# Closing down-projection on one core: the squares of a finished block issued one chunk after its addition to the residual

## The chip, the cores and the metric

The kernel runs on one core of a Trainium2 chip. The metric is the device time of one execution in microseconds (us); before the change three runs gave 2178.75, 2179.22 and 2181.02 us, median 2179.22 us. One further execution was taken by the hardware profiler; it took 2178.91 us, of which the profile's span (first to last instruction) is 2177.0 us.

## The reference, cut to what matters

The program is a two-layer decoder trunk on 256 tokens with model width 2048, in float32: a gMLP token mixer and a convolutional feed-forward network, a shared key/value side, forgetting attention, a second feed-forward network, and a final RMSNorm. The change lies in the end of it:

```python
def rmsnorm(x, g):
    xf = x.astype(jnp.float32)
    r = lax.rsqrt(jnp.mean(xf * xf, axis=-1, keepdims=True) + EPS)
    return (xf * r).astype(x.dtype) * g
...
        h = h + conv_ffn(rmsnorm(h, f_norm[l]), f_w_up[l], f_conv_w[l],
                         f_conv_b[l], f_w_down[l])
...
    return rmsnorm(h, final_norm)
```

So after the last down-projection (a 256 x 5632 by 5632 x 2048 product) each token's row is added to the residual, the sum of its 2048 squares is taken, and the row is multiplied by the gains of the final norm and by one factor per token.

## The kernel before

**A stream of weight chunks.** All weights pass through one loop, `Stream.run`. An item of it is a chunk of weights, 128 partitions x 1024 float32, 512 KB. For item i the loop does four things in the order in which the instructions then stand in every engine's queue: SyncE issues the load of item i + 6 (L78); item i + 3 is *split*, which means that ScalarE rounds the raw chunk `raw` to a part `whi` of lower precision (L110) and VectorE writes the remainder `wlo` = `raw` - `whi` (L111); TensorE multiplies item i (L212: products of the rounded and remainder parts of weights and activations); and then every pending generator is *advanced* to its next `yield`. Generators hold all the other work (evictions from PSUM, norms, attention). A `yield` in such a generator thus means: the rest is issued one chunk later, behind the split of the next item. No scheduler moves anything. Every engine takes its queue in the order in which the loop wrote it.

**Rooms.** There are four `whi` and four `wlo` buffers, so item i + 3 is split into those of item i - 1, as soon as TensorE is done with that item. There are four `raw` buffers.

**The closing stage.** The second down-projection takes the tokens as the stationary operand and makes its output in blocks of 512 columns. Blocks 0, 1 and 2 mix two kinds of items. A *plain* chunk is split as above and gives 24 matrix multiplications of 256 columns. A *seven* chunk is one load but two items: VectorE first makes sums of its weights into a room (L490, L492, L493); the first item is the split of the raw weights (`whi` L88, `wlo` L89, 768 wide, 9 multiplications), the second item the split of the sums (L88 and L89 again, 1024 wide, 12 multiplications). Block 0 has one seven chunk among 22, near its end; blocks 1 and 2 have eight each, in the order plain, plain, seven, plain, seven, plain, plain, seven and so on. Block 3 is two short blocks of 256 columns of plain chunks, and the last of them is written out by a separate function, `output`.

**What happens to a finished block.** The generator `sums_into_residual` adds the seven chunks' sums to the residual `h` in four steps (L569 to L578). Then the generator `final`, for each of the two token halves tb = 0, 1, adds the block's PSUM to `h` on VectorE and squares it on ScalarE with a sum along the row, both issued in one step (`add_block`, L435 and L436); in the next step VectorE multiplies by the gains (L449). Five blocks end like this; the last, in `output`, calls `add_block` too.

**The sums of the activations.** Before the first seven chunk, a generator `all_sums` makes sums of the activation tiles in four rounds (`sums_of_blocks`, L469 to L478): additions on VectorE, then ScalarE rounds the result into a tile (L477) and VectorE writes the remainder (L478). The tile is called X in the profile; it is the stationary operand of the seven chunks.

Of the kernel before, what the change touches and what calls it, by code (L numbers as in the profile page):

```python
# [10 lines left out]
F32 = mybir.dt.float32  # L11
F32R = mybir.dt.float32r
I32 = mybir.dt.int32
AF = mybir.ActivationFunctionType
OP = mybir.AluOpType
AX = mybir.AxisListType

P = 128
D = 2048
T = 256  # L20
# [156 lines left out]
def build(ctx, tc, d, out):  # L177
    nc = tc.nc
# [3 lines left out]
    small = ctx.enter_context(tc.tile_pool(name="small", bufs=1))  # L182
# [228 lines left out]
    def by_token():  # L411

        return h.rearrange("p a b -> p (a b)").rearrange("p (t f) -> p t f", t=2)
# [17 lines left out]
    def add_block(tb, cols, ps, into):  # L431

        hh = by_token()[:, tb, cols]
        sq = small.tile([P, 2, T], F32, name="sq", tag="sq", bufs=2).rearrange("p a b -> p (a b)")
        nc.vector.tensor_tensor(hh, hh, ps, op=OP.add)  # L435
        nc.scalar.activation(sq[:, :ps.shape[1]], hh, AF.Square, accum_out=into)  # L436

    def final(blk):
        def done(ps):
            while state["summed"] < min(blk + 1, 3):  # L440
                yield
            ss = ph.keep("ss", [P, 2, 5])
            n = ps.shape[2]
            cols = slice(blk * 512, blk * 512 + n)
            for tb in range(2):
                add_block(tb, cols, ps[:, tb, :], ss[:, tb, blk:blk + 1])
                yield
                hh = by_token()[:, tb, cols]
                nc.vector.tensor_tensor(hh, hh, ph.keep("gains", [P, D])[:, cols], op=OP.mult)  # L449
                yield  # L450
            if blk == 3:
                v, nv = ph.keep("v", [P, 2]), ph.keep("nv", [P, 2])
                nc.vector.tensor_reduce(v, ss[:, :, :4], axis=AX.X, op=OP.add)
                nc.vector.tensor_scalar(v, v, 1.0 / D, EPS, op0=OP.mult, op1=OP.add)
                nc.vector.tensor_scalar(nv, v, -0.5, None, op0=OP.mult)
                nc.scalar.activation(warm, ones, AF.Sqrt)
        return done

    def block_sums():

        return X1.rearrange("p (q r) w -> p q (r w)", r=2).rearrange("p q (f l t) -> p q f l t", f=4, l=2)

    def sums_of_blocks(q, pair):

        H = ffn_h()
        x, f = (room().rearrange("p (q i t) -> p q i t", q=2, i=4) for _ in range(2))
        hi, lo = (block_sums()[:, q:q + 2, :, i, :] for i in range(2))
        hh = H[:, 2 * pair:2 * pair + 4, :].bitcast(F32)
        nc.vector.tensor_tensor(x.rearrange("p q i t -> p (q i t)").rearrange("p (k t) -> p k t", k=4),  # L469
                                hh[:, :, :T], hh[:, :, T:], op=OP.add)  # L470
        nc.vector.tensor_tensor(f[:, :, :2, :], x[:, :, 1:2, :].to_broadcast([P, 2, 2, P]), x[:, :, 0::3, :],
                                op=OP.subtract)
        yield
        nc.vector.tensor_tensor(f[:, :, 2, :], f[:, :, 1, :], x[:, :, 0, :], op=OP.subtract)
        nc.vector.tensor_tensor(f[:, :, 3, :], f[:, :, 2, :], x[:, :, 2, :], op=OP.add)
        yield
        nc.scalar.activation(hi, f, AF.Copy)  # L477
        nc.vector.tensor_tensor(lo, f, hi.bitcast(F32), op=OP.subtract)  # L478
        yield

    def all_sums():
        for _ in range(4):
            yield
        for q in range(0, len(SUMMED), 2):
            yield from sums_of_blocks(q, SUMMED[q])
# [312 lines left out]
    def ffn_h():  # L798
        ph.open(f"ffn{state['layer']}")
        return ph.keep("H", [P, KF, 2 * T], F32R)  # L800

    def room():
        return ph.temp("room", [P, CHUNK])
# [411 lines left out]
```

## Time and profile before

| | us |
|---|---|
| median of three runs | 2179.22 |
| the profiled execution | 2178.91 |
| its span | 2177.0 |
| TensorE busy | 2165.4 |
| VectorE busy | 1535.1 |
| ScalarE busy | 1163.4 |
| closing stage, about | 1932 to 2169 |

Busy time is the time in which the profile shows at least one instruction on the engine. In the rows of the timeline the columns are: start in us from the span's start, duration in us, engine, source line, operation, output <- inputs, matrix or tile shapes, count (neighbouring instructions of one kind are merged), and in brackets the idle time of the engine just before and what ended it. PE is TensorE, DVE VectorE, ACT ScalarE, SPq the queue of SyncE. In the rows of waits the columns are: the engine and line that waited, the engine and line that it waited for, us in total, how often, the longest.

### The profile page before, as it was taken

To read this page: it belongs to the slowest core of one execution; us is meant where nothing else is said; L and a number is where in the kernel's file an instruction comes from. 1 tells how busy PE (TensorE), PEld (TensorE's weight loads), DVE (VectorE), ACT (ScalarE), POOL (GpSimd) and SP (SyncE) were. 2 spreads that over 40 slices of the span, in tenths; PEclk is the share of its full clock that TensorE was granted. 3 is DMA by queue.
4 is the path that set the end of the run, shared out by engine and by line. 5 is a ranking of instruction groups with operands and counts; after the bars stand their busy time and mean duration, and the time that the engine had idled before them with its cause. 6 is when DMAs were issued, how large, how long until landed. Compare 5 with 4: busy or idle time off the path is not lost.

```text
span 2177.0 us, 45111 instructions
## 1 busy us (share of the span) xinstructions
PE 2165.4 (99%) x18689; PEld 2148.9 (99%) x18689; DVE 1535.1 (71%) x2188; ACT 1163.4 (53%) x1560; POOL 27.4 (1%) x46
## 2 busy tenths in 40 slices
PE   9999999999999999999999999999999999999998
PEld 9999999999999999999999999999999999999998
DVE  6696687777777745556787676678777777778874
ACT  6665555555555544444554665546555555554553
POOL 0000000000000000000001200000000000000000
PEclk9999999999999999999999999999999999999999
DMA  8686565565666566666778776567756565655574
GB/s 312 191 245 200 192 198 194 187 201 188 200 192 195 195 193 195 194 194 184 246 238 263 235 220 199 184 223 220 246 194 194 194 194 187 201 191 177 196 215 153
DMA packets 153230, 447.32 MB, mean 205 GB/s; under 512 B 25584, under 2 KB 44800, under 8 KB 152640
## 3 DMA queue, kind: packets, MB, share of 16 engines
q1 hardware_dynamic: 151488, 440.48, 63.1%
q0 software_dynamic: 1072, 3.41, 0.6%
q8 instruction: 146, 2.39, 0.5%
q10 hardware_dynamic: 464, 0.55, 0.1%
q14 instruction: 60, 0.49, 0.1%
HBM read 430.72 MB, written 13.65 MB: 204 GB/s over the span
## 4 chain that ended last, share of the span: by engine, by line
PE 99%; DVE 1%; DMA 0%; ACT 0%; SPq 0%; issue 0%; DVEq 0%; ACTq 0%
PE ps L212 97%; PE mp L1072 0%; DMA mlp_vt<-a_in_v 0%; DVE wlo L111 0%; ACT whi L110 0%; PE ps L1067 0%; PE ps L1066 0%; PE ps L1065 0%; PE mp L1071 0%; DVE wlo L89 0%; DVE h L435 0%; SPq L78 0%; ACT sq L436 0%; SPq L652 0%; DVE h L647 0%
## 5 line engine op out<-in xcount | busy, mean ns | idle before, releaser
L111 DVE TENSOR_TENSOR wlo<-raw,whi 128x1024 fp32r<-128x1024 f32 x761 | 923.7, 1219 | 390.6 <-ACT whi L110 386.9
L110 ACT ACTIVATE whi<-raw 128x1024 fp32r<-128x1024 f32 x761 | 800.8, 1058 | 674.3 <-PE ps L212 599.2
L212 PE MATMUL ps<-X,whi 128*128 128x256 f32 (+1 forms) x6476 | 824.0, 279 | 0.0
L212 PEld LDWEIGHTS ps<-X,whi 128*128 128x128 f32 x6476 | 776.2, 188 | 6.5
L212 PE MATMUL ps<-X,wlo 128*128 128x256 f32 x3328 | 445.3, 276 | 0.0
L212 PEld LDWEIGHTS ps<-X,wlo 128*128 128x128 f32 x3328 | 409.9, 188 | 1.6
L212 PE MATMUL ps<-whi,ffn_H 128*128 128x256 f32 (+1 forms) x1232 | 201.5, 277 | 0.5 <-ACT whi L110 0.4
L212 PE MATMUL ps<-whi,X 128*128 128x256 f32 (+1 forms) x1136 | 183.1, 279 | 0.4 <-ACT whi L110 0.4
L212 PEld LDWEIGHTS ps<-whi,ffn_H 128*128 128x128 f32 x1232 | 172.9, 188 | 1.3 <-ACT whi L110 0.9
L212 PE MATMUL ps<-ffn_H,whi 128*128 128x256 f32 x1408 | 173.9, 276 | 0.0
L822 DVE SCALAR_TENSOR_TENSOR ffn_room<-ffn_room,col 128x255 f32<-128x255 f32 x352 | 161.8, 481 | 6.4
L212 PEld LDWEIGHTS ps<-ffn_H,whi 128*128 128x128 f32 x1408 | 166.1, 188 | 0.0
L212 PE MATMUL ps<-whi,att_X 128*128 128x256 f32 (+2 forms) x970 | 164.3, 285 | 0.0
L212 PEld LDWEIGHTS ps<-whi,X 128*128 128x128 f32 x1136 | 155.0, 188 | 2.0 <-ACT whi L110 0.6
L212 PE MATMUL ps<-wlo,ffn_H 128*128 128x256 f32 (+1 forms) x615 | 139.2, 277 | 1.5 <-DVE wlo L111 1.5
L212 PEld LDWEIGHTS ps<-whi,att_X 128*128 128x128 f32 x970 | 135.3, 188 | 3.5
L388 DVE TENSOR_TENSOR ffn_room<-ps,rB 128x512 f32<-128x512 f32 x76 | 52.6, 692 | 116.1 <-PE ps L212 116.1
L818 ACT ACTIVATE ffn_room<-ffn_room,col 128x256 f32<-128x256 f32 x176 | 96.3, 595 | 50.0 <-DVE ffn_room L388 50.0
L212 PE MATMUL ps<-wlo,X 128*128 128x256 f32 (+1 forms) x566 | 116.7, 279 | 0.0
L212 PE MATMUL ps<-wlo,att_X 128*128 128x256 f32 (+2 forms) x476 | 105.4, 286 | 0.0
L212 PEld LDWEIGHTS ps<-wlo,ffn_H 128*128 128x128 f32 x615 | 101.1, 188 | 2.0 <-DVE wlo L111 1.9
L212 PE MATMUL ps<-ffn_H,wlo 128*128 128x256 f32 x704 | 94.1, 276 | 0.0
(196 smaller groups left out, 1518.0 us busy)
## 6 DMA issues: line engine op xcount, KB each, us to landing
raw<-up SPq DMA_DIRECT2D x352, 512.0 KB, 4.1
raw<-down SPq DMA_DIRECT2D x154, 512.0 KB, 4.2
raw<-a_in_u SPq DMA_DIRECT2D x32, 512.0 KB, 4.2
raw<-a_out SPq DMA_DIRECT2D x32, 512.0 KB, 3.9
raw<-b_q SPq DMA_DIRECT2D x32, 512.0 KB, 4.5
raw<-kvf_v SPq DMA_DIRECT2D x32, 512.0 KB, 4.9
raw<-b_g SPq DMA_DIRECT2D x32, 512.0 KB, 4.4
raw<-b_out SPq DMA_DIRECT2D x32, 512.0 KB, 4.0
```

The costliest lines, as they stand in the source:

```text
L110: self.nc.scalar.activation(h, raw, AF.Copy)
L111: self.nc.vector.tensor_tensor(l, raw, h.bitcast(F32), op=OP.subtract)
L212: nc.tensor.matmul(o, a, b, start=start, stop=stop, skip_group_check=True)
L388: nc.vector.tensor_tensor(a, src, rB[:, None, :].to_broadcast([P, 2, T]), op=OP.mult)
L818: nc.scalar.activation(c[:, m, :], a[:, m, :], AF.Identity, scale=w[2], bias=column(C_CONVB + l * 2 * KF + f))
L822: nc.vector.scalar_tensor_tensor(c[:, m, n:], a[:, m, :T - n], w[k], c[:, m, n:], op0=OP.mult, op1=OP.add)
```

## The change

Two generators have their `yield` statements moved; no instruction is added or taken away. In `final` the square is issued one chunk after the addition, and the multiplication by the gains in the step after that, together with the addition of the second half. The number of steps is the same. `output` still uses `add_block` as it was. In `sums_of_blocks` the remainder is issued one chunk after the rounding.

```diff
             for tb in range(2):
-                add_block(tb, cols, ps[:, tb, :], ss[:, tb, blk:blk + 1])
-                yield
                 hh = by_token()[:, tb, cols]
+                sq = small.tile([P, 2, T], F32, name="sq", tag="sq", bufs=2).rearrange("p a b -> p (a b)")
+                nc.vector.tensor_tensor(hh, hh, ps[:, tb, :], op=OP.add)
+                yield
+                nc.scalar.activation(sq[:, :n], hh, AF.Square, accum_out=ss[:, tb, blk:blk + 1])
+                yield
                 nc.vector.tensor_tensor(hh, hh, ph.keep("gains", [P, D])[:, cols], op=OP.mult)
-                yield
...
         nc.scalar.activation(hi, f, AF.Copy)
+        yield
         nc.vector.tensor_tensor(lo, f, hi.bitcast(F32), op=OP.subtract)
-        yield
```

Two lines more stand ahead of the later code, so line numbers above L450 are two higher in the changed kernel (L490 becomes L492, L578 becomes L580), the addition L435 is L448 there, the square L436 is L450, and the multiplication by the gains L449 is L452.

ScalarE's queue at the end of block 0, before:

```order
L110 ACTIVATE whi<-raw 128x1024
L436 ACTIVATE sq,ffn_ss<-h 128x512
L88 ACTIVATE whi<-raw 128x768
L88 ACTIVATE whi<-ffn_room 128x1024
L436 ACTIVATE sq,ffn_ss<-h 128x512
L110 ACTIVATE whi<-raw 128x1024 x2
```

and now:

```order
L110 ACTIVATE whi<-raw 128x1024
L88 ACTIVATE whi<-raw 128x768
L450 ACTIVATE sq,ffn_ss<-h 128x512
L88 ACTIVATE whi<-ffn_room 128x1024
L110 ACTIVATE whi<-raw 128x1024
L450 ACTIVATE sq,ffn_ss<-h 128x512
```

Each square stands one rounding later: the first behind the rounding of the next seven chunk's raw weights, the second behind the rounding of the plain chunk that follows that seven chunk. The end of block 1 reads the same.

VectorE's queue at the same place, before (`ffn_room` is the room of the weight sums):

```order
L435 TENSOR_TENSOR h<-h,ps 128x512
L490 TENSOR_TENSOR ffn_room<-raw 128x512
L492 TENSOR_TENSOR ffn_room<-raw,ffn_room 128x256
L493 TENSOR_TENSOR ffn_room<-raw,ffn_room 128x256
L89 TENSOR_TENSOR wlo<-raw,whi 128x768
L449 TENSOR_TENSOR h<-h,ffn_gains 128x512
L89 TENSOR_TENSOR wlo<-ffn_room,whi 128x1024
L435 TENSOR_TENSOR h<-h,ps 128x512
L111 TENSOR_TENSOR wlo<-raw,whi 128x1024
L449 TENSOR_TENSOR h<-h,ffn_gains 128x512
L111 TENSOR_TENSOR wlo<-raw,whi 128x1024
```

and now:

```order
L448 TENSOR_TENSOR h<-h,ps 128x512
L492 TENSOR_TENSOR ffn_room<-raw 128x512
L494 TENSOR_TENSOR ffn_room<-raw,ffn_room 128x256
L495 TENSOR_TENSOR ffn_room<-raw,ffn_room 128x256
L89 TENSOR_TENSOR wlo<-raw,whi 128x768
L89 TENSOR_TENSOR wlo<-ffn_room,whi 128x1024
L452 TENSOR_TENSOR h<-h,ffn_gains 128x512
L448 TENSOR_TENSOR h<-h,ps 128x512
L111 TENSOR_TENSOR wlo<-raw,whi 128x1024 x2
L452 TENSOR_TENSOR h<-h,ffn_gains 128x512
```

Both multiplications by the gains stand one remainder later; the additions stay where they were.

The last of the four rounds of activation sums, on VectorE, before:

```order
L475 TENSOR_TENSOR ffn_room<-ffn_room 128x2x128
L111 TENSOR_TENSOR wlo<-raw,whi 128x1024
L478 TENSOR_TENSOR X_74<-ffn_room,X_74 128x8x128
L490 TENSOR_TENSOR ffn_room<-raw 128x512
L492 TENSOR_TENSOR ffn_room<-raw,ffn_room 128x256
L493 TENSOR_TENSOR ffn_room<-raw,ffn_room 128x256
L89 TENSOR_TENSOR wlo<-raw,whi 128x768
L89 TENSOR_TENSOR wlo<-ffn_room,whi 128x1024
```

and now:

```order
L477 TENSOR_TENSOR ffn_room<-ffn_room 128x2x128
L111 TENSOR_TENSOR wlo<-raw,whi 128x1024
L492 TENSOR_TENSOR ffn_room<-raw 128x512
L494 TENSOR_TENSOR ffn_room<-raw,ffn_room 128x256
L495 TENSOR_TENSOR ffn_room<-raw,ffn_room 128x256
L89 TENSOR_TENSOR wlo<-raw,whi 128x768
L481 TENSOR_TENSOR X_74<-ffn_room,X_74 128x8x128
L89 TENSOR_TENSOR wlo<-ffn_room,whi 128x1024
```

The remainder X of the last round moved from ahead of the first seven chunk's weight sums to between its two weight remainders; in the first three rounds it moved behind one more `wlo` of a plain chunk. The queues of TensorE, GpSimd and SyncE are the same in both kernels.

More of the change, by code (lines that the diff above doesn't have):

```diff
@@ L445, in done @@
             for tb in range(2):
-                add_block(tb, cols, ps[:, tb, :], ss[:, tb, blk:blk + 1])
+                hh = by_token()[:, tb, cols]
+                sq = small.tile([P, 2, T], F32, name="sq", tag="sq", bufs=2).rearrange("p a b -> p (a b)")
+                nc.vector.tensor_tensor(hh, hh, ps[:, tb, :], op=OP.add)
                 yield
-                hh = by_token()[:, tb, cols]
+                nc.scalar.activation(sq[:, :n], hh, AF.Square, accum_out=ss[:, tb, blk:blk + 1])
+                yield
                 nc.vector.tensor_tensor(hh, hh, ph.keep("gains", [P, D])[:, cols], op=OP.mult)
-                yield
             if blk == 3:
```

## The prediction, made before the change was run

> **What bounds the kernel now.** I read the page first, then the waits of TensorE after 1900 us, then that engine's busy time in windows.
>
> ```profile
> span 2177.0 us, 45111 instructions
> PE 2165.4 (99%) x18689; PEld 2148.9 (99%) x18689; DVE 1535.1 (71%) x2188; ACT 1163.4 (53%) x1560; POOL 27.4 (1%) x46
> ...
> PE 99%; DVE 1%; DMA 0%; ACT 0%; SPq 0%; issue 0%; DVEq 0%; ACTq 0%
> ```
> ```profile
> PE ps L212 <- DVE wlo L111: 1.5, 2, 0.8
> PE ps L212 <- ACT whi L110: 0.4, 1, 0.4
> ```
> ```profile
> 1940.00:1980.00 40.00, 40.00 (x355) 40.00 (x355) 34.21 (x39) 19.93 (x20) 0.00 (x0) 1.00 0.62 204
> ...
> 2003.00:2007.00 4.00, 3.12 (x26) 2.73 (x25) 2.25 (x4) 3.36 (x5) 0.00 (x0) 1.00 0.20 79
> 2007.00:2061.00 54.00, 54.00 (x479) 54.00 (x478) 46.68 (x60) 27.63 (x30) 0.00 (x0) 1.00 0.63 206
> 2061.00:2066.00 5.00, 3.85 (x31) 3.45 (x31) 3.26 (x5) 3.35 (x5) 0.00 (x0) 1.00 0.30 97
> 2066.00:2120.00 54.00, 54.00 (x479) 54.00 (x479) 44.24 (x54) 28.06 (x30) 0.00 (x0) 1.00 0.71 216
> ```
>
> TensorE is the bound everywhere: 11.6 us of the span are outside its busy time. What the change can win is only what TensorE waits in the closing stage, and that is two places, the ends of blocks 0 and 1; the windows ahead, between and behind are full. The second number of a window is TensorE's busy time; the granted clock (third number from the end) is 1.00 in all five. Here are the two places on TensorE:
>
> ```profile
> 2004.77 0.89 PE L212 MATMUL ps<-whi,ffn_H 128*128 128x256 f32 x3
> 2006.42 0.50 PE L212 MATMUL ps<-wlo,ffn_H 128*128 128x256 f32 x2 [0.76 <-DVE wlo L111]
> ...
> 2063.31 0.28 PE L212 MATMUL ps<-whi,ffn_H 128*128 128x256 f32 x1
> 2063.98 0.50 PE L212 MATMUL ps<-whi,ffn_H 128*128 128x256 f32 x2 [0.39 <-ACT whi L110]
> 2065.24 0.50 PE L212 MATMUL ps<-wlo,ffn_H 128*128 128x256 f32 x2 [0.76 <-DVE wlo L111]
> ```
>
> In both, the last multiplication of a seven chunk (2004.77, the first of the three; 2063.31) is followed by a plain chunk, call it c: two multiplications with `whi`, then `wlo`. The pitch is 54.00 us / 479 = 0.113 us, so without a wait `wlo` of c would begin 3 x 0.113 = 0.34 us after the seven chunk's last one: at 2005.11 and 2063.65. It began at 2006.42 and 2065.24, that is **1.31 and 1.59 us late, 2.90 us together**.
>
> By busy time the loss reads smaller: 4.00 - 3.12 = 0.88 and 5.00 - 3.85 = 1.15 us, 2.03 together. In the Trainium skill, the page "Perfetto Trace Analysis" (opening note) calls matmul busy time a bad metric because matmuls are pipelined; the trace agrees, with 0.28 us shown for a multiplication whose pitch is 0.113 us, and by busy time the sum below would give 2.0 instead of 2.9 us. I take the starts, since they are what moves the end.
>
> Why c's remainder was late, on ScalarE and then VectorE:
>
> ```profile
> 1994.93 1.06 ACT L110 ACTIVATE whi<-raw 128x1024 fp32r<-128x1024 f32 x1 [1.66 <-PE ps L212]
> 1998.61 0.63 ACT L436 ACTIVATE sq<-h 128x512 f32<-128x512 f32 x1 [2.62 <-DVE h L435]
> ...
> 1999.24 0.83 ACT L88 ACTIVATE whi<-raw 128x768 fp32r<-128x768 f32 x1
> 2000.22 1.06 ACT L88 ACTIVATE whi<-ffn_room 128x1024 fp32r<-128x1024 f32 x1
> 2003.43 0.63 ACT L436 ACTIVATE sq<-h 128x512 f32<-128x512 f32 x1 [2.15 <-DVE h L435]
> ...
> 2004.06 1.99 ACT L110 ACTIVATE whi<-raw 128x1024 fp32r<-128x1024 f32 x2
> ```
> ```profile
> 1997.89 0.69 DVE L435 TENSOR_TENSOR h<-h,ps 128x512 f32<-128x512 f32 x1
> 1998.50 0.68 DVE L490 TENSOR_TENSOR ffn_room<-raw 128x512 f32<-128x512 f32 x1
> ...
> 1999.67 0.43 DVE L493 TENSOR_TENSOR ffn_room<-raw,ffn_room 128x256 f32<-128x256 f32 x1
> 2000.11 0.96 DVE L89 TENSOR_TENSOR wlo<-raw,whi 128x768 fp32r<-128x768 f32 x1
> 2000.98 0.69 DVE L449 TENSOR_TENSOR h<-h,ffn_gains 128x512 f32<-128x512 f32 x1
> 2001.58 1.22 DVE L89 TENSOR_TENSOR wlo<-ffn_room,whi 128x1024 fp32r<-128x1024 f32 x1
> 2002.72 0.68 DVE L435 TENSOR_TENSOR h<-h,ps 128x512 f32<-128x512 f32 x1
> 2005.14 1.23 DVE L111 TENSOR_TENSOR wlo<-raw,whi 128x1024 fp32r<-128x1024 f32 x1 [1.75 <-ACT whi L110]
> ```
>
> ```profile
> ACT sq L436 <- DVE h L435: 26.3, 10, 4.8
> ```
>
> Every one of the ten squares waits for its addition. The second square waits for the second addition (2002.72 + 0.68 = 3.40). Queued behind it is the rounding of c, first of the two at 2004.06. VectorE, done at 2003.40, idles 1.75 us for it, and writes c's remainder from 2005.14 to 2006.37. So the two engines wait for each other in turn.
>
> **The change, part by part.** It removes and adds no instruction, and TensorE's, SyncE's and GpSimd's queues are unchanged. *Squares.* I walk the end of block 0 in the new order. c's `whi` needs a buffer that the item four earlier frees. That is the previous seven chunk's second item:
>
> ```profile
> 1998.09 0.28 PE L212 MATMUL ps<-whi,X 128*128 128x256 f32 x1
> ...
> 1999.67 0.50 PE L212 MATMUL ps<-whi,ffn_H 128*128 128x256 f32 x3
> ```
>
> It ends at 1999.78 (one pitch after 1999.67), and the plain chunk before that seven chunk ended six multiplications ahead of 1998.09, near 1997.4, which is when L88 (raw) may start. No longer behind the square, it is done by 1998.3, or, if it waits until L490 shows at 1998.50 that the load is there, by 1999.4 with the first square behind it done at 2000.0; either way ahead of what follows. The weight sums end at 1999.67 + 0.43 = 2000.10. Then, step by step: rounding of the sums 2000.12 to 2001.18; VectorE's remainder of the sums 2001.20 to 2002.42; 1.14 us after its start (2001.58 to 2002.72) the multiplication by the gains at 2002.34; 0.60 us after that (2000.98 to 2001.58) the second addition at 2002.94 to 2003.62; 0.60 us later c's remainder, 2003.54 to 2004.77. Its rounding ran from 2001.2 to 2002.2, with nothing in front. TensorE wants it at 2005.11: 0.34 us to spare, so all of 1.31 us is won.
>
> At the end of block 1 the same sums of weights end later against TensorE:
>
> ```profile
> 2058.49 0.43 DVE L493 TENSOR_TENSOR ffn_room<-raw,ffn_room 128x256 f32<-128x256 f32 x1
> ```
>
> 2058.92 + the same steps (2004.77 - 2000.10 = 4.67) gives 2063.59 for c's remainder, wanted at 2063.65: 0.06 us to spare. So 1.59 us, less nothing to 0.2.
>
> *What is late next.* Behind the second square now stands the rounding of c + 1: square at 2003.65, the rounding 0.63 us later (1998.61 to 1999.24), 2004.28 to 2005.34, the remainder 2005.36 to 2006.58; TensorE wants it one plain chunk (24 x 0.113 = 2.71) after 2005.11, at 2007.82. The seven chunk behind it is tighter, for VectorE has no idle time there:
>
> ```profile
> 2006.89 1.22 DVE L111 TENSOR_TENSOR wlo<-raw,whi 128x1024 fp32r<-128x1024 f32 x1
> ...
> 2010.84 1.23 DVE L89 TENSOR_TENSOR wlo<-ffn_room,whi 128x1024 fp32r<-128x1024 f32 x1 [0.34 <-ACT whi L88]
> ...
> 2069.66 1.23 DVE L89 TENSOR_TENSOR wlo<-ffn_room,whi 128x1024 fp32r<-128x1024 f32 x1 [0.34 <-ACT whi L88]
> ```
>
> Before, its second remainder was written at 2012.07, and wanted at 2006.42 + 2 x 2.71 + 9 x 0.113 - 0.113 = 2012.75: 0.68 us to spare, and by the same sum 0.68 at 2070.89. VectorE's queue from there on moves up by 0.9 us (the weight sums start 0.60 + 1.14 after 2005.36, at 2007.10; before, 1.14 after 2006.89, at 2008.03), TensorE by 1.31 and 1.59. That leaves 0.3 us at block 0 and about zero at block 1. So I take 0.05 us off for both thin places, with 0 to 0.4 as bounds.
>
> At the end of block 2 the change wins nothing: TensorE is busy all of 2066 to 2120 already. The loads are no cover that could fail:
>
> ```profile
> raw<-down SPq DMA_DIRECT2D x154, 512.0 KB, 4.2
> ```
>
> c's load goes into the `raw` buffer of the chunk four loads earlier, which was split ahead of the split at 1994.93, and lands 4.2 us after its issue, so by about 1999.5 at the latest; its rounding now begins at 2001.2.
>
> *Sums of the activations.* I cost this edit at nothing. VectorE's L478 (1.22 us) moves behind the weight sums of the first seven chunk and ahead of its second remainder:
>
> ```profile
> 1975.75 1.22 DVE L478 TENSOR_TENSOR X<-ffn_room,X 128x1024 fp32r<-128x1024 f32 x1
> ...
> 1978.95 1.06 ACT L88 ACTIVATE whi<-ffn_room 128x1024 fp32r<-128x1024 f32 x1 [1.87 <-PE ps L212]
> ...
> 1980.05 1.23 DVE L89 TENSOR_TENSOR wlo<-ffn_room,whi 128x1024 fp32r<-128x1024 f32 x1 [0.69 <-ACT whi L88]
> ```
>
> Its cover is VectorE's wait of 0.69 us there and the three chunks by which splits run ahead. Without the 0.69, the second remainder would be later by at most 1.22 us; a split that begins when TensorE lets it (1978.95) is wanted two plain chunks and a seven chunk's first item later, 2 x 2.71 + 1.02 = 6.4 us, so even that reaches no multiplication. A gain is excluded too: TensorE is busy for all 40 us of the window 1940 to 1980.
>
> **The sum:** -1.31 - 1.59 + 0.05 = -2.85 us. The profiled execution goes from 2178.91 to about 2176.06. It lay 0.31 us below the median, so the time I predict is 2179.22 - 2.85 = **2176.4 us**, 0.13% less. About 0.2% (4.4 us) is what a measurement of this kernel can tell from no change, so this counts as no change. The costs cannot make it a gain over 0.2%: all waits of TensorE in the stage sum to 2.90.
>
> **The rivals.** *A thin place breaks.* One of the two places at block 1 has 0.06 us and the other about none. For it: these are sums of many rows. Against: after each, VectorE catches up, since a wait of TensorE gives it time. If the second place keeps half of its wait (0.8 us), the time is 2179.22 - 2.90 + 0.8 = 2177.1; I let this stand for 2177.0 to 2178.5. *Nothing comes out of it:* VectorE, not the square, sets c's remainder (46.68 of 54 us busy, and it must do the same work). Then c's remainder stays at 2005.14, and the time at 2179.2. Against it: the 1.75 us that VectorE idles directly in front of it. *Slower:* the second square now parks in front of the rounding of c + 1, and holds it until the second addition is done. In the walk it holds it from 2002.2 to 2003.65, 1.45 us, which is in the sum already. If the addition ends later by x, c + 1's remainder and the tight seven chunk behind it are later by x, and TensorE waits x - 0.3 us at block 0 and x at block 1. From x = 1.6 us on that is more than the 2.90 won. With the longest hold that a square shows, 4.8 us, x is 4.8 - 1.45 = 3.35 and the time 2179.22 - 2.90 + 3.05 + 3.35 = 2182.7. For it: VectorE is busy for nearly all of the time ahead of the addition. Against it: the change takes waits out of that queue and adds none.
>
> **How the numbers follow.** Forecast 0.70 (2175.6 to 2177.0 with the spread of runs), thin place 0.14, nothing 0.11, slower 0.05. The range 2175.3 to 2179.2 holds all of the first two and half of the third. Faster by over 0.2%, below 2174.9, could only come from the runs' own spread (2178.75 to 2181.02): 0.05. Slower by over 0.2%, above 2183.6: 0.03. Within: 0.92.
>
> **What would show it.** Right: the windows around 2004 and 2062 read full, L111 of c shows no wait for `whi` L110, and the total that squares wait for additions (26.3 us) falls; the end of TensorE comes 2.9 us earlier, and the tail behind it, 2169.4 to 2177.0, is the same.
>
> Wrong: a wait of TensorE for `wlo` L89 or L111 some 5 to 8 us behind either place, or a wait at the first seven chunk, near 1985.

## The result, and the profile after

| | before | after |
|---|---|---|
| median, us (22 runs each) | 2179.45 | 2175.85 |
| lowest and highest, us | 2178.42, 2183.68 | 2174.96, 2178.51 |
| the profiled execution, us | 2178.91 | 2175.67 |
| its span, us | 2177.0 | 2173.8 |
| start of TensorE's last multiplication, us | 2169.06 | 2165.81 |

The ratio after to before is 0.9981, with a 95% interval of 0.9975 to 0.9988. The kernel is faster, by 0.19%. That is just under the 0.2% that I had set as the bound of what can be told; with 22 runs each the interval excludes 1, so the bound was set too wide. The forecast was 2176.4 us, 0.5 us above the measured median.

The page of the kernel after, its first lines and its chain of waits:

```profile
span 2173.8 us, 45113 instructions
...
PE 2164.6 (100%) x18689; PEld 2149.0 (99%) x18689; DVE 1536.1 (71%) x2188; ACT 1162.4 (53%) x1560; POOL 26.4 (1%) x46
...
PE 100%; DVE 0%; ACT 0%; POOL 0%; issue 0%; DVEq 0%; POOLq 0%
```

The chain lost VectorE's 1%. The list of TensorE's waits behind 1900 us, which had three waits in it, is empty. The two windows that read 3.12 of 4.00 and 3.85 of 5.00 are now full (second number: TensorE's busy time, with its count of multiplications; third from the end: granted clock):

```profile
2003.00:2007.00 4.00, 4.00 (x37) 4.00 (x37) 3.40 (x5) 2.41 (x4) 0.00 (x0) 1.00 0.45 137
...
2060.00:2066.00 6.00, 6.00 (x56) 6.00 (x55) 5.33 (x9) 2.48 (x5) 0.00 (x0) 1.00 0.57 173
```

The squares' waits for their additions, in ScalarE's waits behind 1900 us (26.3 us in ten waits before). L436 is now only the last block's, in `output`:

```profile
ACT sq L436 <- DVE h L435: 8.0, 2, 4.8
ACT sq L450 <- DVE h L448: 3.1, 2, 1.5
```

ScalarE and VectorE at the end of block 0, after:

```profile
1997.53 0.85 ACT L88 ACTIVATE whi<-raw 128x768 fp32r<-128x768 f32 x1 [1.66 <-PE ps L212]
1998.49 0.63 ACT L450 ACTIVATE sq<-h 128x512 f32<-128x512 f32 x1
...
2000.09 1.06 ACT L88 ACTIVATE whi<-ffn_room 128x1024 fp32r<-128x1024 f32 x1 [0.88 <-DVE ffn_room L495]
2001.05 1.05 ACT L110 ACTIVATE whi<-raw 128x1024 fp32r<-128x1024 f32 x1
2003.64 0.63 ACT L450 ACTIVATE sq<-h 128x512 f32<-128x512 f32 x1 [1.54 <-DVE h L448]
...
2004.27 1.04 ACT L110 ACTIVATE whi<-raw 128x1024 fp32r<-128x1024 f32 x1
```
```profile
2001.18 1.23 DVE L89 TENSOR_TENSOR wlo<-ffn_room,whi 128x1024 fp32r<-128x1024 f32 x1 [0.34 <-ACT whi L88]
2002.33 0.69 DVE L452 TENSOR_TENSOR h<-h,ffn_gains 128x512 f32<-128x512 f32 x1
2002.93 0.68 DVE L448 TENSOR_TENSOR h<-h,ps 128x512 f32<-128x512 f32 x1
2003.53 1.22 DVE L111 TENSOR_TENSOR wlo<-raw,whi 128x1024 fp32r<-128x1024 f32 x1
2005.35 1.23 DVE L111 TENSOR_TENSOR wlo<-raw,whi 128x1024 fp32r<-128x1024 f32 x1 [0.60 <-ACT whi L110]
...
2007.09 0.69 DVE L492 TENSOR_TENSOR ffn_room<-raw 128x512 f32<-128x512 f32 x1
```

The rounding of c (L110) starts at 2001.05, with nothing in front, where it started at 2004.06. So c's remainder (L111) begins at 2003.53 without a wait, where VectorE had idled 1.75 us and begun at 2005.14. TensorE, at both places, passes from the seven chunk into c without a break; its `wlo` starts at 2004.99 and 2062.11:

```profile
2004.65 0.50 PE L212 MATMUL ps<-whi,ffn_H 128*128 128x256 f32 x3
2004.99 0.39 PE L212 MATMUL ps<-wlo,ffn_H 128*128 128x256 f32 x2
...
2061.77 0.50 PE L212 MATMUL ps<-whi,ffn_H 128*128 128x256 f32 x3
2062.11 0.39 PE L212 MATMUL ps<-wlo,ffn_H 128*128 128x256 f32 x2
```

Two multiplications with `wlo` take 0.39 us here; in the rows of before, behind each wait, they take 0.50. So a wait costs 0.11 us more than the lateness of the multiplication that waited: the step behind it is twice as long. I had missed that.

**The account by starts.** From the start times of the single multiplications in each trace I added up, behind 1998 us, what steps of over 150 ns are longer than the usual 113.33 ns (waits), and what steps between 115 and 122 ns are longer than it (long pitch, explained below). The last columns are the time from the 17,500th multiplication before the end to the last one, against the kernel after, and the same from the first two columns. All in us; the experiments follow below.

```
                     waits  long pitch  last 17,500    more than after   waits + long pitch
before                3.12        0.01      2022.40               3.12                 3.13
after                 0           0.01      2019.28               -                    0.01
squares_only          0.21        0.03      2019.53               0.25                 0.24
sums_only             2.43        2.24      2023.95               4.67                 4.67
second_square_only    0           0         2019.28               0                    0
first_square_only     3.77        4.08      2027.13               7.85                 7.85
later_by_0_6          0.94        6.05      2026.26               6.98                 6.99
later_by_1_8          3.80        6.07      2029.16               9.88                 9.87
```

The two columns account for all of it within 0.02 us. Between the profiled executions of before and after, 3.12 us of the difference is the two places alone: 1.42 us at block 0 and 1.70 at block 1. Another 0.12 us lay ahead of the last 17,500 multiplications, and so ahead of the closing stage.

### The profile page after: what moved, and what is told of

Read it like the earlier page. It is cut to its first block, busy times and chain, and to the rows that moved or that the text cites. A ratio compares the mean times of both kernels' runs of the same rounds, so it can differ in the third digit from the quotient of the medians.

```text
span 2173.8 us, 45113 instructions
## 1 busy us (share of the span) xinstructions
PE 2164.6 (100%) x18689; PEld 2149.0 (99%) x18689; DVE 1536.1 (71%) x2188; ACT 1162.4 (53%) x1560; POOL 26.4 (1%) x46
## 4 chain that ended last, share of the span: by engine, by line
PE 100%; DVE 0%; ACT 0%; POOL 0%; issue 0%; DVEq 0%; POOLq 0%
PE ps L212 98%; PE mp L1074 0%; PE mp L682 0%; PE ps L1068 0%; PE ps L1069 0%; PE ps L1067 0%; PE mp L1073 0%; DVE h L649 0%; PE mp L407 0%; ACT sq L436 0%; PE mp L212 0%; DVE h L435 0%; DVE h L644 0%; ACT fin_t L636 0%; POOL ident L1109 0%
## 5 line engine op out<-in xcount | busy, mean ns | idle before, releaser
L111 DVE TENSOR_TENSOR wlo<-raw,whi 128x1024 fp32r<-128x1024 f32 x761 | 925.0, 1221 | 387.9 <-ACT whi L110 383.4
L110 ACT ACTIVATE whi<-raw 128x1024 fp32r<-128x1024 f32 x761 | 800.7, 1058 | 680.0 <-PE ps L212 592.8
```

The source lines that it names most:

```text
L110: self.nc.scalar.activation(h, raw, AF.Copy)
L111: self.nc.vector.tensor_tensor(l, raw, h.bitcast(F32), op=OP.subtract)
```

## The experiments

**One part at a time.** The theory: the second square, parked in front of the rounding of c, causes both waits; the sums of the activations are worth nothing. The main rival: VectorE's order, not the square, sets c's remainder. The four kernels shared one set of runs of before: median 2179.28 us of 33, from 2177.80 to 2185.83.

Squares parted, sums of the activations as before:

```diff
         nc.scalar.activation(hi, f, AF.Copy)
-        yield
         nc.vector.tensor_tensor(lo, f, hi.bitcast(F32), op=OP.subtract)
+        yield
```
(against the changed kernel)

> Only the squares are parted from their additions; the sums of the activations are as before. Theory (the squares win all of it): TensorE's two waits at the ends of blocks 0 and 1 (1.31 and 1.59 us by starts) are gone and the time is 2.9 us under before, the same as with the whole change. Rival (the parted roundings of the activation sums carry part of the gain): less than 2 us under before, and a wait of TensorE is left near 2004 or 2062.

Measured: 2176.22 us (2175.14 to 2176.96, 11 runs), ratio 0.9980 [0.9972, 0.9989]. The list of TensorE's waits in the closing stage is empty; by starts, two steps from 2062.87 on are longer by 0.21 us together. So the squares carry what is won. That small wait stands at block 1, where the prediction had left 0.06 us to spare; in the kernel after it is missing, and the walk at block 1 below says what differs.

Only the sums of the activations:

```diff
         nc.scalar.activation(hi, f, AF.Copy)
-        nc.vector.tensor_tensor(lo, f, hi.bitcast(F32), op=OP.subtract)
         yield
+        nc.vector.tensor_tensor(lo, f, hi.bitcast(F32), op=OP.subtract)
```

> Only the rounding and the remainder of the activation sums are parted; the squares stay with their additions. Theory: no change (within 0.4 us of before), TensorE still waits twice for wlo L111, 0.76 us each, behind the two seven chunks. Rival (the sums carry part of the gain): 1 us or more under before.

Measured: 2178.96 us (2177.72 to 2182.10), ratio 0.9997 [0.9988, 1.0006]. The two waits of TensorE for `wlo` are as before:

```profile
PE ps L212 <- DVE wlo L111: 1.5, 2, 0.8
```

Only the second square one chunk later (the `yield`s of the first half as before):

```diff
                 nc.vector.tensor_tensor(hh, hh, ps[:, tb, :], op=OP.add)
-                yield
+                if tb == 1:
+                    yield
                 nc.scalar.activation(sq[:, :n], hh, AF.Square, accum_out=ss[:, tb, blk:blk + 1])
                 yield
                 nc.vector.tensor_tensor(hh, hh, ph.keep("gains", [P, D])[:, cols], op=OP.mult)
+                if tb == 0:
+                    yield
```
(against the changed kernel, with the sums of the activations as before)

> Only the square of the second token half is issued one chunk after its addition; the first half is as before, and so are the activation sums. Theory (the second square alone held the rounding of the plain chunk): that rounding needs no square in front any more, the remainder L111 follows the second addition directly, from about 0.6 us after the addition's start, and all of the 2.9 us is won. Rival (both squares share the loss, half each): about 1.5 us under before.

Measured: 2175.54 us (2175.41 to 2176.56), ratio 0.9979 [0.9971, 0.9988], and no wait of TensorE in the closing stage. The second square, moved by one rounding, does everything that the change does. The second multiplication by the gains moves by one step with it, but it stands behind c's remainder in both orders, and VectorE's order ahead of that remainder is the one of before. So the rival that VectorE's order sets c's remainder falls.

Only the first square one chunk later: the same edit with `tb == 0` and `tb == 1` exchanged.

> Only the square of the first token half is issued one chunk after its addition; the second square is issued with its addition as before. Theory: the second addition ends 0.2 us later than before (at 3.62 instead of 3.40 us behind 2000), the rounding of the plain chunk still stands behind the second square, and both waits of TensorE stay and grow by 0.2 us: 0.4 us over before, within 0.6 us of it in any case. Rival (both squares share the loss): about 1.5 us under before.

Measured: 2183.52 us (2180.44 to 2184.62), ratio 1.0012 [1.0003, 1.0021]: slower by 4.2 us, ten times what I had expected. TensorE's waits, and ScalarE's timeline at block 0:

```profile
PE ps L212 <- DVE wlo L111: 1.5, 2, 0.8
PE ps L212 <- ACT whi L110: 1.2, 2, 0.7
```
```profile
2000.92 1.06 ACT L88 ACTIVATE whi<-ffn_room 128x1024 fp32r<-128x1024 f32 x1 [0.88 <-DVE ffn_room L498]
2004.47 0.63 ACT L451 ACTIVATE sq<-h 128x512 f32<-128x512 f32 x1 [2.49 <-DVE h L448]
...
2005.10 1.04 ACT L110 ACTIVATE whi<-raw 128x1024 fp32r<-128x1024 f32 x1
```

The mechanism is as expected: the second square still parks in front of the rounding of c, a little later than before, and by starts the waits grew from 3.12 to 3.77 us. That is 0.65 of the 4.2. The rest is not in any wait of its trace. It shows only when two windows of full TensorE time are compared; first_square_only, then after:

```profile
2070.00:2125.00 55.00, 55.00 (x469) 55.00 (x468) 43.42 (x51) 28.39 (x31) 0.00 (x0) 1.00 0.69 211
2125.00:2160.00 35.00, 35.00 (x299) 35.00 (x298) 18.07 (x21) 16.37 (x21) 0.00 (x0) 1.00 0.58 179
```
```profile
2070.00:2125.00 55.00, 55.00 (x487) 55.00 (x487) 43.60 (x51) 28.62 (x32) 0.00 (x0) 1.00 0.74 220
2125.00:2160.00 35.00, 35.00 (x311) 35.00 (x310) 16.54 (x19) 15.03 (x18) 0.00 (x0) 1.00 0.46 138
```

Both are busy throughout at a granted clock of 1.00, but one does 469 multiplications in 55 us and the other 487: 117.3 against 112.9 ns. By starts the pitch behind the second place is 117.78 ns there and 113.33 ns in after, to the last multiplication. This **long pitch** cost 4.08 us. In sums_only it lasted from the first place to the second and cost 2.24 us; TensorE came to the second place later by that, and so its wait there was shorter, 2.43 us in all instead of 3.12:

```profile
2009.00:2060.00 51.00, 51.00 (x435) 51.00 (x435) 42.66 (x54) 26.64 (x29) 0.00 (x0) 1.00 0.66 206
2070.00:2125.00 55.00, 55.00 (x488) 55.00 (x487) 43.56 (x52) 30.10 (x34) 0.00 (x0) 1.00 0.72 218
```

**Is it the wait that brings the long pitch?** The new theory: a wait of TensorE can leave its stream of 256-column multiplications at the long pitch until the next wait or until wider multiplications come. So an execution of the kernel before would be 2.3 us (first place), 4 us (second) or 6.3 us longer than its best, by chance. That would fit the spread of its runs, but no trace of before shows it in the closing stage. The rival: the extra time of such runs has another cause, and the pitch belongs to the order of the instructions. The next four kernels shared 21 runs of before: median 2179.95 us, from 2177.97 to 2184.16.

Before, with eight of c's twelve pairs of products made 512 columns wide instead of twice 256, and two in the next plain chunk:

```diff
                 yield
+            if blk < 2:
+                between()
             if blk == 3:
```

> The kernel before, and in the plain chunk at which TensorE waits (the one behind the second seven chunk of blocks 1 and 2) the first 8 of its 12 products are one multiplication of 512 columns instead of two of 256, and 2 in the next plain chunk; the columns and the result are the same. The two waits stay. Theory (a wait may leave TensorE at a pitch of 117.8 instead of 113.3 ns until it is disturbed again, and multiplications of 512 columns behind it bring the short pitch back): the profile shows 113.3 ns behind both waits, and the times keep to within 1.5 us of 2178.3, without the ones at 2181 to 2186 that before shows. Rival (the wide multiplications do nothing to the pitch): the same spread as before, with about a third of the runs above 2180.5.

Measured: 2179.07 us (2178.15 to 2179.48, 11 runs), ratio 0.9994 [0.9985, 1.0003]. The waits are those of before (1.5 us for `wlo`, 0.4 for `whi`), and behind both the pitch is 113.33 ns. No run lies above 2179.5, while 9 of 21 of before lie above 2180.4. That is what the theory expects: the best runs stay where they were, and the long ones are gone. The ratio alone does not tell the two kernels apart.

After, with bursts of VectorE additions in the two up-projections that make TensorE wait some twenty times:

```diff
+    def burst():
+        sq = small.tile([P, 2, T], F32, name="sq", tag="sq", bufs=2).rearrange("p a b -> p (a b)")
+        for _ in range(14):
+            nc.vector.tensor_tensor(sq, col[:, :512], col[:, :512], op=OP.add)
+        for _ in range(3):
+            yield
...
+            if i % 4 == 3 and i < 43:
+                s.then(at_mult=lambda: s.start(burst()))
```

> The changed kernel with 14 additions of 512 columns more on VectorE (their result is not used) behind every fourth of 44 column blocks of both up-projections, 8.4 us each time, so that TensorE waits once or twice for a remainder at each of 22 places, some 1 to 3 us. Theory (each wait draws one of the two pitches by chance): several of the 22 stretches between them run at 117.8 ns, the others at 113.3. Rival (the long pitch belongs to the closing stage's seven chunks): all 22 at 113.3 ns.

Measured, one profiled execution: 2298.9 us.

```profile
PE ps L212 <- DVE wlo L111: 74.5, 20, 5.8
```

The waits were longer than I had meant (3.7 us on average, not 1 to 3), and behind each of them multiplications ran at nearly twice the pitch, 213 ns, for some 3 to 6 us; the mean granted clock fell to 0.977. The edit makes ten bursts in each up-projection, so there are 20 places and not the 22 of the expectation. Where the stream came back to speed, it was at 117.78 ns behind two of the 20 waits (those ending at 334 and 1772 us) and at 113.33 behind the others, fewer than the "several" that I expected. So the long pitch is not tied to the closing stage, and most waits do not bring it.

The same with wide products behind each burst (in that phase `between()` is called after every burst's chunk):

> As the run with many waits, and in the chunk at which TensorE waits the first 8 rounded products are multiplications of 512 columns, 2 in the next. Theory (wide multiplications behind a wait bring the short pitch back): all 22 stretches at 113.3 ns. Rival: as many at 117.8 ns as without them.

Measured: 2300.62 us, waits 72.2 us in 20, and the long pitch behind six of them, so the expectation fell. The trace tells why this tells little against the theory: in these phases a chunk's products with `whi` come first, and the eight wide ones were among them, ahead of the wait for `wlo`; the two in the next chunk ran at half speed (427 ns each) behind 18 of the 20 waits, ahead of the point where the pitch settled. There is support of another kind in the same traces. Three long stretches end at 512-column products with no wait near, one in many_waits (1806.45 us) and two here (1945.90 and 2057.36), and the 256-column multiplications behind all three run at 113.3 ns.

After, with three additions of 128x512 on VectorE ahead of the second addition of blocks 0 and 1, so that it comes 1.8 us later:

```diff
+                if tb == 1 and blk < 2:
+                    for _ in range(3):
+                        nc.vector.tensor_tensor(sq, hh, hh, op=OP.add)
                 nc.vector.tensor_tensor(hh, hh, ps[:, tb, :], op=OP.add)
```

> The changed kernel with three additions of 512 columns more on VectorE (0.6 us apart, result unused) ahead of the second addition at the ends of blocks 0 and 1, so that the plain chunk's remainder is later by 1.8 us. By the trace of the changed kernel it had 0.24 and 0.24 us to spare. Theory: TensorE waits for it 1.6 us at each place, and nothing more behind it (the seven chunk behind has TensorE's wait as its own time won): 3.2 us over the changed kernel, 2179.1, plus 2 to 6 us in those executions in which a wait leaves the long pitch. Rival (VectorE's late queue costs TensorE again at the next seven chunks): two or more waits behind each place, 5 us or more in waits.

Measured: 2182.00 us (2180.18 to 2185.95, 11 runs), ratio 1.0014 [1.0005, 1.0023].

```profile
PE ps L212 <- DVE wlo L111: 3.2, 2, 1.8
```

The waits came as expected, 1.6 us on average by this view (1.8 and 1.4), 3.80 us together by starts. In the profiled execution a step of 135 ns from 2013.74 to 2013.87, in the seven chunk behind, was followed by the long pitch, which stood again behind the second wait, to the last multiplication: 6.07 us.

**Wide products behind a wait, and a small wait.** The last two kernels shared 21 runs of before, with a median of 2182.82 us (2178.30 to 2185.09). Only one of these 21 lies below 2180, so the long times are far more frequent in this set than in the others (the three sets ran on three chips), and ratios of different sets are not to be compared to a microsecond.

later_by_1_8 with the wide products of squares_early_wide:

> As the run with the remainder later by 1.8 us (2182.0 us, 2180.2 to 2186.0), and the plain chunk at which TensorE waits has 8 of its 12 products as one multiplication of 512 columns, 2 in the next. Theory (a wait can leave a pitch of 117.8 ns, and multiplications of 512 columns right behind the wait bring 113.3 back): the waits stay at 3.2 us of idle time, the pitch is 113.3 behind both, and the times lie closely around 2175.85 + 3.8 = 2179.6, none above 2181. Rival (the spread of that run has another cause, loads or clock): a spread of 4 us or more as without them, and a median near 2182.

Measured: 2183.12 us (2180.23 to 2185.16), ratio 1.0000 [0.9992, 1.0009]. The pitch was 113.33 ns behind both places, as expected, but the times fell out as the rival had them: a median near 2183 and a spread of 4.9 us, where I had expected 2179.6 and none above 2181. The waits read 3.7 us. Window and timeline of TensorE behind the first place:

```profile
2007.00:2012.00 5.00, 4.22 (x15) 3.60 (x16) 4.33 (x7) 2.24 (x5) 0.00 (x0) 0.66 0.58 160
```
```profile
2007.78 0.50 PE L212 MATMUL ps<-wlo,ffn_H 128*128 128x512 f32 x1 [1.84 <-DVE wlo L111]
2008.11 0.97 PE L212 MATMUL ps<-whi,ffn_H 128*128 128x512 f32 x2
2008.88 0.63 PE L212 MATMUL ps<-wlo,ffn_H 128*128 128x512 f32 x1
2009.31 1.05 PE L212 MATMUL ps<-whi,ffn_H 128*128 128x512 f32 x2
```

The granted clock is 0.66 in this window: from 2008.46 on single steps of 512 columns take 427 ns, against 231 to 236 at full clock, for about 3 us, and the same again from 2069.69. In this execution one cost was taken away and another came in its place; whether it is the same in the other ten runs no trace shows.

After, with one such addition instead of three, so that the second addition is 0.6 us later:

> The changed kernel with one addition of 512 columns more on VectorE (0.6 us, result unused) ahead of the second addition at the ends of blocks 0 and 1. The spare time by the trace of the changed kernel is 0.24 us at each. Theory: TensorE waits 0.4 us at each place, 0.8 to 1.0 us in all, so 2176.8 in executions with the short pitch; those in which a wait leaves the long pitch are 2.3 us (first place) or 4.0 us (second place, up to the end) slower, 2179 to 2183. Rival (the spare time is larger than read, or a short wait never leaves the long pitch): within 1.2 us of the changed kernel in every execution.

Measured: 2181.11 us (11 runs), ratio 0.9988 [0.9979, 0.9997]. The runs form two groups: three from 2177.05 to 2177.53, and eight from 2180.83 to 2182.02, nothing between. Waits, timeline and windows of TensorE in the profiled execution, one of the long ones:

```profile
PE ps L212 <- DVE wlo L111: 0.4, 1, 0.4
```
```profile
2011.11 0.39 PE L212 MATMUL ps<-whi,X 128*128 128x256 f32 x2
2011.33 0.32 PE L212 MATMUL ps<-wlo,X 128*128 128x256 f32 x1
2011.49 0.40 PE L212 MATMUL ps<-whi,X 128*128 128x256 f32 x2
```
```profile
2007.00:2012.00 5.00, 5.00 (x46) 5.00 (x45) 4.59 (x7) 2.74 (x3) 0.00 (x0) 1.00 0.70 228
2012.00:2060.00 48.00, 48.00 (x410) 48.00 (x409) 40.38 (x53) 24.91 (x28) 0.00 (x0) 1.00 0.65 201
```

The multiplication behind the one at 2011.33 was held for 49 ns (it starts 162 ns behind it). Ahead of it the pitch is short in spite of the wait at 2004; from it on the window does 48 / 410 = 117.1 ns. So a hold of 49 ns can be enough. It cost 1.98 us up to the wait at 2064; behind that wait the long pitch stood again, to the last multiplication, for another 4.07. Together that is 6.05 us, where the waits themselves cost 0.94. That the group of short times has the short pitch is inferred; no trace of one was taken.

## Why the prediction was right, and where its size was off

*What bounds the kernel.* Right. Nothing but TensorE's waits at the two places moved: the tail behind the last multiplication's start is 7.9 us before (2177.0 - 2169.06) and 8.0 after (2173.8 - 2165.81).

*The cause.* Right, and shown by second_square_only (all of it) against first_square_only and sums_only (nothing won). By this the first square need not have moved: second_square_only has the same time and, as the thin places below show, more to spare.

*The walk at block 0.* Right to 0.03 us in every step: rounding of the sums 2000.12 (measured 2000.09), gains 2002.34 (2002.33), second addition 2002.94 (2002.93), c's remainder 2003.54 (2003.53), c + 1's square, rounding and remainder 2003.65, 2004.28 and 2005.36 (2003.64, 2004.27, 2005.35), weight sums 2007.10 (2007.09). The first square also stands where the walk had it, right behind L88 (1998.49), and did not delay anything. TensorE itself ran 0.12 us earlier, so 0.24 us was to spare instead of 0.34.

*The walk at block 1.* Here the size was off on the safe side. c's remainder:

```profile
2060.65 1.22 DVE L111 TENSOR_TENSOR wlo<-raw,whi 128x1024 fp32r<-128x1024 f32 x1
2062.47 1.23 DVE L111 TENSOR_TENSOR wlo<-raw,whi 128x1024 fp32r<-128x1024 f32 x1 [0.60 <-ACT whi L110]
```

It ended at 2061.87 and was wanted at 2062.11: 0.24 to spare, not 0.06. The walk had taken over from before that the weight sums of block 1 end later against TensorE; in after they do not. What differs is the plain chunk ahead of that place, whose rounding waits for TensorE, in squares_only and then in after:

```profile
2053.09 1.06 ACT L110 ACTIVATE whi<-raw 128x1024 fp32r<-128x1024 f32 x1 [1.94 <-PE ps L212]
2051.93 1.06 ACT L110 ACTIVATE whi<-raw 128x1024 fp32r<-128x1024 f32 x1 [1.65 <-PE ps L212]
```

In squares_only it begins 2.87 us ahead of TensorE's next multiplication with X (2055.96), in after 3.15 us (2055.08). At block 0 it is 3.15 in both. All five traces with the sums of the activations as before have the 2.87, and the four with parted sums and the short pitch there have 3.15. So it is the edit of the sums that gave block 1 these 0.28 us; without them squares_only waits 0.21 us at 2062.87. Why an edit some 75 us earlier does that, no run shows.

*The thin places.* I had feared the seven chunk behind each place, with 0.3 us to spare at block 0 and none at block 1. In after, the remainder of the sums and the first multiplication that reads it are, at block 0:

```profile
2009.91 1.23 DVE L89 TENSOR_TENSOR wlo<-ffn_room,whi 128x1024 fp32r<-128x1024 f32 x1 [0.34 <-ACT whi L88]
2011.33 0.28 PE L212 MATMUL ps<-wlo,X 128*128 128x256 f32 x1
```

The remainder ends 0.20 us ahead of the multiplication, at block 1 as well; before it was 0.82 us at both. Where the closing stages of these traces have 0.18 us or more here, the step behind that multiplication is regular. It is 131 ns at 0.15 us (squares_only, 2069.57), 135 ns at 0.14 (later_by_1_8, 2013.74) and 162 ns at 0.12 (later_by_0_6, 2011.33). So this remainder is most likely what holds TensorE there, though the list of waits does not name it, and after stands some 0.05 us from such a hold. second_square_only has 0.53 and 0.25 us there.

*The terms of the sum.* -1.31 and -1.59 were mis-sized: 1.42 and 1.70 us by starts, since I took the lateness at the start of c's first `wlo` and left out the step behind it, 221 and 222 ns instead of 113. By busy time it would have been 0.88 and 1.15, so starts were the better measure, but to be complete they must be counted until the pitch is regular again. Together that is 3.12 us, not 2.90. The +0.05 for thin places did not show in after. The term of zero for the sums of the activations was right by itself: 2178.96 against 2179.28 us, with an interval that holds 1. Beside the parted squares it is the 0.2 us at block 1 by the traces, too little for the times to tell.

*From the profiled execution to the median.* The forecast carried the 0.31 us between the profiled execution and the median of before over unchanged: 2176.06 + 0.31. After's profiled execution took 2175.67, 0.39 us less than forecast, and lies 0.18 us below its median, so this step was off by 0.13 us only. That is luck: against the median of 22 runs before's profiled execution lies 0.54 us low, and the profiled difference is 3.24 us where that of the medians is 3.60. Before's profiled execution had the short pitch behind both waits; 8 of its 22 runs lie above 2180, and only one of the 22 of after lies above 2177. That these runs of before had the long pitch is inferred, from the sizes of their excess and from sums_only, which keeps both waits and whose trace shows it. A trace of such a run of before I do not have. Why one run of after took 2178.51 us is open.

*The rivals.* "Nothing" and "thin place breaks" did not come. The slower rival was not seen either, but later_by_1_8 puts its price to the test: for x = 1.8 its price is 1.5 and 1.8 us of waits; measured by starts they were 2.10 and 1.69. The place was another than I had said. VectorE's addition stands ahead of c's own remainder, so TensorE waits at c, and the seven chunk behind then gets by with a step of 135 ns. The prediction put the point from which the change would lose at x = 1.6. Against before in the same sets, the change with x = 0.6 still wins (0.9988) and with x = 1.8 loses (1.0014), so the point lies between them, as far as two sets with unlike shares of long times can tell. The long pitch, which the prediction did not know, adds up to 6 us to such waits: at x = 0.6 eight of eleven runs took 2180.8 us and more.

## What to carry to other kernels

Where two in-order engines wait for each other in turn, issue the dependent instruction one step later, behind the work that does not depend on it; here one moved instruction was worth the whole change. Count what an engine at the bound loses by the starts of its instructions, through the step behind the wait, and compare instruction counts of equally full windows, since "100% busy at clock 1.00" hid a pitch 4% longer. A wait of TensorE, however short, may cost far more than its length, so a thin place is worth making a few tenths of a microsecond safe.

## What the runs showed of the hardware that I had not expected

**Two pitches.** A stream of weight loads and 128x256 multiplications ran at 113.33 ns or at 117.78 ns each, at the same granted clock of 1.00. In the stages looked at above the long one set in behind disturbances between about 22 ns (the 135 ns step of later_by_1_8) and some 6 us, and not behind each of them; it lasted up to 108 us (later_by_0_6, from the wait at 2064 to the last multiplication at 2172), and ended only at the next wait or at 512-column multiplications. But a disturbance is not needed. In all twelve traces, that of the kernel after included (992.90 to 998.56), 48 such multiplications at a change of the operands, with `whi` and X behind `ffn_H` and `wlo`, run at 117.9 ns, directly behind steps of 113 to 115 ns, until multiplications of another width come. So the long pitch belongs in some places to the order of the instructions and follows a wait in others, in some executions. What decides between the two is open.

**The halved clock came early.** In later_by_1_8_wide, gaps of 2.2 us between starts at 2005.55 and 2066.42 were each followed, 0.7 and 1.1 us after the end of the gap, by some 3 us at half speed. In the profile of later_by_1_8 gaps of 2.1 and 1.7 us were not. In many_waits all 20 gaps, of 3.1 to 6.0 us, were followed by 3 to 6 us of it, while of four gaps of 3.3 us in many_waits_wide two were followed by it and two by none. The Trainium skill, page "TensorE: Matmul & The Clock Gate", section "What's actually happening", puts the fall to half rate behind at least one idle window of about 3.4 us; by that rule a gap of 2.2 us would cost nothing more, and here the measurement differs: the length of the gap alone does not decide.
